# Issuing the stores of gates and of block one's split weight parts from GpSimd's queue, in a one-core streaming encoder layer

## The chip, the cores and the metric

The kernel runs on one core of one Trainium2 chip. The metric is device time of one execution in microseconds; lower is better. The profile calls the engines PE (TensorE's matmuls), PEld (TensorE's weight loads), DVE (VectorE), ACT (ScalarE), POOL (GpSimd) and SP (SyncE, which here only issues transfers). A "q" behind a name, as in SPq, is that engine's queue of instructions.

## The reference

One layer of a chunk-causal encoder on a prompt of 2048 frames and a sample of 64 frames, width 1024, all in fp32. Cut to what matters:

```python
h = rms_norm(x, p['norm1_g']) * (1 + sc1) + sh1
z = h @ p['w_in']
glu_a, glu_b, q, k, v, g_conv, g_attn = jnp.split(z, offs, axis=-1)
u = glu_a * jax.nn.sigmoid(glu_b)
conv_out, conv_state = conv_module(u, ...)      # causal depthwise conv, 31 taps; layer norm; swish; projection
q, k = rms_norm(q), rms_norm(k)                 # per head
attn_out = attend(q, k, v, rel_bias) @ p['w_attn_out']   # each chunk of 64 sees itself and 8 before it
merged = jax.nn.sigmoid(g_conv) * conv_out + jax.nn.sigmoid(g_attn) * attn_out
x = x + gt1 * (merged @ p['w_o'])
h2 = rms_norm(x, p['norm2_g']) * (1 + sc2) + sh2
gate, up = jnp.split(h2 @ p['w_ffn_in'], 2, axis=-1)
x = x + gt2 * ((jax.nn.silu(gate) * up) @ p['w_ffn_out'])
```

Shifts, scales and gates (sh, sc, gt) come from a small conditioning vector. The states of convolution, keys and values are outputs too.

## The kernel before, in words

**Precision.** Products are made in a fast 32-bit format. Each fp32 operand is split into a high part, a copy rounded to that format (`whi`, made on ACT), and a low part, the rest (`wlo`, a subtraction on DVE or POOL); three products, high by high, high by low and low by high, are summed in PSUM (`mm3`).

**Two phases.** The first phase walks over four blocks of tokens (`PBLOCKS`, 576 then three times 512). In each block TensorE makes, in this order: queries, one part of the gated convolution input, keys, another part, values, two more parts, and then the 16 columns of gates (`ORDER`). Attention of the block runs in between. Results that the second phase needs go to DRAM: queries, keys, values, attention (`o_d`), convolution (`c_d`) and the gates (`g_d`). The second phase walks over three blocks (`CBLOCKS`), merges, projects and runs the feed-forward part, with seven products of half-size blocks in place of eight.

**Weights.** Class `Weights` hands out the split weights in the order of use. A raw weight is loaded into a staging buffer (`wst`, three of them at first), split into `whi` and `wlo` (five pairs are held), and used. Weights that a later block uses again, those of the first phase and five of the feed-forward part (`KEPT`), are split once: `then` at lines 511 to 517 stores both parts to DRAM (`w_din_h`, `w_din_l`, `w_dqkv_h` and so on; the store is line 515), and the later blocks load them back (line 480). A part's pair of buffers is free again when TensorE has used it and its store has landed. The store is written down a little after the split (`stream.at`).

**Gates.** `gates` at lines 1389 to 1421 makes each gate column in parts of 288 tokens (block zero), or of 512 or 256: eight or more products into a PSUM bank, a tanh on ACT into a buffer of the tag `t` (seven buffers, lines 776 to 779, which other temporaries share), and a store into `g_d`, line 1399. The second phase loads the gates at line 1133.

**What sets the order.** TensorE's order is written out by hand: the program walks through the work with a running estimate of each engine's load (`Stream`, `Meter`) and interleaves several lists of work (`Lane`). `Meter` lets `dma_start` through without counting it. The other queues are filled by the framework from this program; every queue then runs in order. An instruction that waits holds up what stands behind it in the same queue. SP's queue holds nearly all transfers: loads of weights (line 385 and line 480), of queries and keys for attention (1464, 1465), of values (1471, 1473), of the attention bias (1517), of rows of x for the next block's norm (1146 and 1159), and stores of convolution results (1363), attention (1495), keys and queries (1026), values (1053). ACT's queue holds its own activations and the gates' stores. POOL's queue holds no transfer before the change. Its work in the first phase: the root `r` of the norms of queries, keys and rows of x (`rsqrt_mean`), the sums `s` of the convolution's norm, copies of the convolution's history (`hist`), and some low parts of weights (`wlo`).

Every operation that the program issues through `Meter` has line 106 in the profile; so groups there are told apart by the names of the tiles.

Of the kernel before, what the change touches and what calls it, by code (L numbers as in the profile page):

```python
# [8 lines left out]
F32 = mybir.dt.float32  # L9
# [54 lines left out]
KEPT = ("qkv", "in", "fi")  # L64
# [205 lines left out]
class Weights:  # L270
# [4 lines left out]

    def __init__(self, engines, pool, dram, stream, keys, source, staging, held, kept):
        self.stream = stream
        self.sync, self.act, self.dve, self.gps = engines
        self.pool, self.dram, self.keys, self.source = pool, dram, keys, source

        self.staging, self.held, self.reach = staging, held, 0
        self.sum_pool, self.sum_d, self.sums, self.early, self.landed = None, None, {}, False, {}
        self.behind = nullcontext

        self.room, self.leaving = {"wst": 1, "wup": 0, "wfo": 0}, {"wst": 0, "wup": 0, "wfo": 0}
        times, raws = {}, {}
        self.items, self.users, self.need, self.first, self.stored, self.spread = [], [], {}, set(), {}, set()

        def item(key):
            self.items.append(key)  # L290
            self.users.append(0)
            return len(self.items) - 1

        for i, key in enumerate(keys):
            n = times[key] = times.get(key, 0) + 1
            if key[0] == "up" and n == 1:
                self.first.add(i)
                cs = [c for f, op in key[1:] for c in self.columns_of(f, op)]
                for c in cs:
                    if c not in raws:  # L300
                        raws[c] = item(("fi", c))
                self.need[i] = sorted({raws[c] for c in cs})
                for f, op in key[1:]:
                    for c in self.parts_of(f, op):
                        self.users[raws[c]] += 1
            elif key[0] == "dn":
                fs = [key[:3], (*key[:2], key[2] + 1)]
                for f in fs:
                    if f not in raws:
                        raws[f] = item(("fo", f[2]))  # L310
                self.need[i] = [raws[f] for f in fs]
                for op in key[3:]:
                    for e in self.rows_of(op):
                        self.users[raws[fs[e]]] += 1
            elif n == 1 or not kept(key) or n == 2 and key[:2] == ("qkv", 0):
                self.need[i] = [item(key)]
                self.users[self.need[i][0]] += 1
                if key[0] == "fo" and key[1] in last_rows(0) and n == 1:
                    self.spread.add(self.need[i][0])
        self.raws = raws  # L320
        self.again = {key for key, n in times.items() if n > 1 and kept(key)}
        self.loaded, self.ready, self.used, self.freed, self.given = {}, [], 0, 0, 0

        self.extra = {"wst": staging - 1, "wup": 1, "wfo": 2}

        self.tags = {"fo": (), "": ("wst", "wup", "wfo")}
        self.due = {kind: [] for kind in self.tags}
        for i, key in enumerate(self.items):
            self.due[self.kind(key)].append(i)
        due = self.due[""]  # L330
        for c in (0, FFN):
            due.remove(raws[c])
            due.insert(due.index(self.need[keys.index(("fi", 3 * P))][0]), raws[c])
        self.load_on("")
# [130 lines left out]
    def split(self):  # L465
        i = len(self.ready)
        key = self.keys[i]
        its = self.need.get(i, ())
        if key[0] == "dn":
            shape = [P, len(key) - 3, 512]  # L470
        elif i in self.first:
            shape = [P, 4 * len(key) - 4, P]
        else:
            shape = list(self.loaded[its[0]][0].shape) if its else self.stored[key][1]
        hi = self.pool.tile(shape, F32R, tag="whi", name="whi", bufs=self.held)
        lo = self.pool.tile(shape, F32R, tag="wlo", name="wlo", bufs=self.held)
        self.ready.append((hi, lo))
        if not its:
            for t, d in zip((hi, lo), self.stored[key][0]):
                self.sync.dma_start(t.bitcast(F32), d)  # L480
            return
        turn = {"wo": key[1], "fi": key[1] // P if key[0] == "fi" else 0}.get(key[0], 0)

        passing = key[:2] == ("qkv", 0) and i < 4
        on_dve = ( key[0] == "in" or key[0] == "qkv" and (passing or key[1]) or turn % 2)
        if key[0] == "dn":
            parts = [(slice(j, j + 1), self.second(key, op)) for j, op in enumerate(key[3:])]
            self.stream.after("act", "pool")
        elif i in self.first:
            parts = [(slice(4 * j, 4 * j + 4), self.operand(f, op)) for j, (f, op) in enumerate(key[1:])]  # L490
            self.stream.after("act", "pool")
        else:
            n = 4 if key[0] == "fi" else shape[1]
            parts = [(slice(j, j + n), self.loaded[its[0]][0][:, j : j + n]) for j in range(0, shape[1], n)]
        for c, src in parts:

            late = key[0] in ("up", "fo") and key[1] != (0, "s1") and self.stream.load["pool"] - self.stream.load["pe"] > POOL_BEHIND
            e, name = (self.dve, "dve") if on_dve or late else (self.gps, "pool")
            self.act.activation(hi[:, c], src, AF.Copy)
            self.stream.after(name, "act")  # L500
            e.tensor_tensor(lo[:, c], src, hi[:, c].bitcast(F32), ALU.subtract)
        if i in self.first:
            its = [self.raws[c] for f, op in key[1:] if op[0] == "a" for c in self.parts_of(f, op)]
        if key[0] == "dn":
            its = [self.raws[*key[:2], key[2] + int(op[1]) - 1] for op in key[3:] if op[0] == "b"]
        for j in its:
            self.drop(j, name)
        if key[0] == "dn" and key[3] == "b11":
            self.sum_second(key)

        def then():
            if key in self.again and key not in self.stored and not passing:
                ds = [self.dram.tile(shape, F32, name="w_d" + "_".join(map(str, key)) + "_" + part) for part in "hl"]
                for t, d in zip((hi, lo), ds):
                    self.sync.dma_start(d, t.bitcast(F32))
                self.stored[key] = ds, shape
            self.presum()

        self.stream.at(self.stream.when(name), then, True)
# [104 lines left out]
def streaming_layer(ctx: ExitStack, tc: tile.TileContext, I, O):  # L624
    nc = tc.nc
    stream = Stream()
# [762 lines left out]
    def gates(b, free):  # L1389

        o = PBLOCKS[b][0]
        w = PBLOCKS[b][1] - o

        def part(g, ws, c0, c1):
            ps = columns(*ws, kts(hh), kts(hl), c0, c1)
            t = temp("gate")
            stream.after("act", "pe")
            act.activation(t[:, : c1 - c0], ps[:, : c1 - c0], AF.Tanh, scale=0.5)
            nc.scalar.dma_start(g_d[g // 8, g % 8, :, o + c0 : o + c1], t[:, : c1 - c0])

        def pair(g):
            ws = [W.get(("in", 2560 + g * P, h)) for h in range(2)]
            return [[[w[l][:, k, e * P : e * P + P] for w in ws for k in range(4)] for l in range(2)] for e in range(2)]

        n = 16 - SPLIT_G if b + 1 < len(PBLOCKS) else 16
        for g in range(0, n, 2):
            for e, ws in enumerate(pair(g)):
                for c in halves(0, w):
                    part(g + e, ws, *c)
                if e:  # L1410
                    W.done()
                    W.done()
                yield g + e
        rest = [ws for g in range(n, 16, 2) for ws in pair(g)]
        for c0, c1 in ((0, w // 2), (w // 2, w)):
            for i, ws in enumerate(rest):
                part(n + i, ws, c0, c1)
                if c1 == w and i % 2:
                    W.done()
                    W.done()  # L1420
            free["columns"] = c1
# [265 lines left out]
    M = Slabs(nc.sync, nc.scalar, wa, stream, list(mod_order()), source, 4)  # L1687
    xs = first_columns()
    next(vectors_)
    W = Weights((nc.sync, act, dve, gps), wpool, dram, stream, list(weight_order()), source, 3, 5, lambda key: key[0] in KEPT)  # L1690
    M.fill()
    ordered = ExitStack()
    ordered.enter_context(tc.manual_schedule(engines={mybir.EngineType.PE}))
# [259 lines left out]
    c0, c1 = tile_chunks(*CBLOCKS[0])  # L1953
# [517 lines left out]
```

## Time and profile before

| What | us |
|---|---|
| runs of the kernel before, median of 3 | 2938.12 (2931.04 to 2940.68) |
| the profiled execution, its own time | 2935.84 |
| its span | 2934.1 |
| PE busy in the span | 2877.2 |
| DVE, ACT, POOL busy | 2044.7, 1366.9, 1170.4 |

The profiled execution is one run; its own time holds the span and about 1.7 us around it. Busy time counts when an engine works, not when it works at its best. "Idle before, releaser" names what ended an idle stretch. Where a wait needs several events, the one that came last is named, and it is inferred.

### The profile page before, as it was taken

Reading aid. Unit: us, or ns where it says so; the run is one execution under the profiler, and the core shown is the slowest. Engines: PE = TensorE matmul, PEld = TensorE weight load, DVE = VectorE, ACT = ScalarE, POOL = GpSimd, SP = SyncE. Lnnn points to the kernel's source line nnn. Section 1 sums busy time; section 2 is a strip of 40 time slices with the busy share of each in tenths; the row PEclk is TensorE's granted clock in tenths of the full one; section 3 lists DMA queues with packets and bytes.
Section 4 is the critical chain, followed back from the end, with each engine's and each line's share of the span. In section 5 each row is a group of like instructions: output and inputs, shape, how many; then the busy total and the mean of one; then the engine's idle time right before and its main releaser. Section 6 shows DMA issues by size and latency. Waiting matters only on the chain.

```text
span 2934.1 us, 44538 instructions
## 1 busy us (share of the span) xinstructions
PE 2877.2 (98%) x16130; PEld 2578.7 (88%) x16130; DVE 2044.7 (70%) x3621; ACT 1366.9 (47%) x2441; POOL 1170.4 (40%) x742
## 2 busy tenths in 40 slices
PE   8998999999999999999999999999999999999999
PEld 6798878788888888898999998999999999999998
DVE  5995688578867886487777756666666557566666
ACT  4345634661465267464434345444444345444442
POOL 1301310101011102454566452366667742465767
PEclk9998999999999999999999999999999999999999
DMA  8989889988997897884444876232333965333333
GB/s 320 331 299 320 278 284 307 288 282 288 292 309 233 298 272 238 287 311 166 147 144 144 290 253 215 94 125 87 115 123 104 344 223 180 97 101 108 115 107 127
DMA packets 313788, 634.28 MB, mean 216 GB/s; under 512 B 36864, under 2 KB 133664, under 8 KB 313568
## 3 DMA queue, kind: packets, MB, share of 16 engines
q1 hardware_dynamic: 300464, 612.88, 63.3%
q10 hardware_dynamic: 13104, 18.56, 1.8%
q8 instruction: 127, 2.08, 0.3%
q14 instruction: 93, 0.76, 0.1%
HBM read 482.81 MB, written 148.51 MB: 215 GB/s over the span
## 4 chain that ended last, share of the span: by engine, by line
PE 48%; DVE 2%; ACT 1%; issue 0%; POOL 0%; ACTq 0%; DVEq 0%
PE ps L106 29%; PE pd L106 14%; PE pw L106 5%; DVE wlo L106 1%; DVE pw L106 0%; ACT whi L106 0%; DVE ps L106 0%; DVE t L106 0%; DVE sums L106 0%; PE pt L106 0%; DVE acc L106 0%; ACT xn L106 0%; DVE hid L106 0%; ACT hid L106 0%; DVE b L106 0%
## 5 line engine op out<-in xcount | busy, mean ns | idle before, releaser
L106 PE MATMUL ps<-t,whi 128*128 128x384 f32 (+1 forms) x2112 | 502.1, 322 | 2.1 <-ACT u L106 0.8
L106 POOL TENSOR_TENSOR wlo<-wst,whi 128x1024 fp32r<-128x1024 f32 (+1 forms) x159 | 363.2, 2296 | 239.9 <-ACT whi L106 204.8
L106 ACT ACTIVATE whi<-wst 128x1024 fp32r<-128x1024 f32 (+1 forms) x265 | 257.9, 978 | 294.4 <-PE ps L106 126.7
L106 PE MATMUL ps<-b,whi 128*128 128x384 f32 (+1 forms) x1584 | 378.4, 324 | 4.8 <-DVE v L106 2.1
L106 PEld LDWEIGHTS ps<-t,whi 128*128 128x128 f32 x2112 | 367.6, 188 | 9.5 <-ACT u L106 3.0
L106 DVE SCALAR_TENSOR_TENSOR y<-u,wd,y 128x512 f32<-128x512 f32 (+1 forms) x480 | 369.3, 773 | 7.7
L106 PE MATMUL ps<-hh,whi 128*128 128x512 f32 (+2 forms) x992 | 364.2, 367 | 0.0
L106 DVE TENSOR_TENSOR acc<-acc,pd 128x512 f32<-128x512 f32 x482 | 322.3, 685 | 48.6 <-PE pd L106 46.1
L106 PE MATMUL ps<-hh,wlo 128*128 128x512 f32 (+2 forms) x992 | 346.3, 349 | 0.0
L106 PE MATMUL ps<-hl,whi 128*128 128x512 f32 (+2 forms) x992 | 345.9, 349 | 0.0
L106 PE MATMUL ps<-t,wlo 128*128 128x384 f32 (+1 forms) x1056 | 338.2, 321 | 0.0
L106 PE MATMUL pd<-whi,hid 128*128 128x512 f32 x912 | 297.3, 391 | 0.3 <-DVE hid L106 0.3
L106 PEld LDWEIGHTS ps<-b,whi 128*128 128x128 f32 x1584 | 275.6, 188 | 12.9 <-DVE v L106 3.2
L106 ACT ACTIVATE pr<-pr,sm 128x640 f32<-128x640 f32 (+3 forms) x272 | 202.5, 749 | 154.4 <-DVE sm L106 152.3
L106 PE MATMUL ps<-b,wlo 128*128 128x384 f32 (+1 forms) x792 | 255.0, 322 | 0.0
L106 POOL TENSOR_TENSOR r<-t,mhalf 128x8 f32<-128x8 f32 (+4 forms) x54 | 86.3, 1599 | 395.6 <-DVE t L106 385.4
L106 PEld LDWEIGHTS ps<-hh,wlo 128*128 128x128 f32 x992 | 188.0, 189 | 23.1
L106 PEld LDWEIGHTS ps<-hh,whi 128*128 128x128 f32 x992 | 188.6, 190 | 17.3 <-issue 2.5
L106 PEld LDWEIGHTS pd<-whi,hid 128*128 128x128 f32 x912 | 171.1, 188 | 36.3 <-ACT hid L106 0.7
L106 DVE TENSOR_TENSOR wlo<-wst,whi 128x1024 fp32r<-128x1024 f32 (+1 forms) x106 | 134.5, 1276 | 97.6 <-ACT whi L106 96.4
L106 PEld LDWEIGHTS ps<-hl,whi 128*128 128x128 f32 x992 | 188.9, 190 | 14.8 <-issue 1.7
L106 PEld LDWEIGHTS ps<-t,wlo 128*128 128x128 f32 x1056 | 198.1, 188 | 0.8
(235 smaller groups left out, 6274.6 us busy)
## 6 DMA issues: line engine op xcount, KB each, us to landing
whi<-w_din_h SPq DMA_DIRECT2D x72, 512.0 KB, 6.1
wlo<-w_din_l SPq DMA_DIRECT2D x72, 512.0 KB, 6.9
wst<-sum_d SPq DMA_DIRECT2D x131, 256.0 KB, 2.9
wfo<-in_w_ffn_out SPq DMA_DIRECT2D x64, 512.0 KB, 3.9
sum_d<-ws SPq DMA_DIRECT2D x88, 256.0 KB, 2.2
wst<-in_w_ffn_in SPq DMA_DIRECT2D x85, 256.0 KB, 2.9
wst<-in_w_ca SPq DMA_DIRECT2D x35, 512.0 KB, 5.2
wst<-in_w_ffn_in SPq DMA_DIRECT2D x35, 512.0 KB, 4.6
```

The costliest lines, as they stand in the source:

```text
L106: self.last = f(*args, **kw)
```

## The change

Two groups of stores are issued from another queue. The stores of both parts of a weight that is used again (line 515) move from SP's queue to GpSimd's; the stores of the gates (line 1399) move from ACT's queue to GpSimd's. Sources, destinations, sizes and the arithmetic stay the same. `Weights` gets the plain GpSimd engine as a fifth engine, beside the metered one.

```diff
-        self.sync, self.act, self.dve, self.gps = engines
+        self.sync, self.act, self.dve, self.gps, self.other = engines
...
                 for t, d in zip((hi, lo), ds):
-                    self.sync.dma_start(d, t.bitcast(F32))
+                    self.other.dma_start(d, t.bitcast(F32))
...
             act.activation(t[:, : c1 - c0], ps[:, : c1 - c0], AF.Tanh, scale=0.5)
-            nc.scalar.dma_start(g_d[g // 8, g % 8, :, o + c0 : o + c1], t[:, : c1 - c0])
+            nc.gpsimd.dma_start(g_d[g // 8, g % 8, :, o + c0 : o + c1], t[:, : c1 - c0])
...
-    W = Weights((nc.sync, act, dve, gps), wpool, dram, stream, list(weight_order()), source, 3, 5, lambda key: key[0] in KEPT)
+    W = Weights((nc.sync, act, dve, gps, nc.gpsimd), wpool, dram, stream, list(weight_order()), source, 3, 5, lambda key: key[0] in KEPT)
```

## The prediction, made before the changed kernel ran

> **What bounds the kernel now.** I read the page first, then the stages, then what TensorE waits for, and last the queue that the moved stores stand in now (SP) and the one that they go to (GpSimd's, which the profile calls POOL). The stages below come from the windows view: stretch, its length, busy time of PE, weight loads, VectorE (DVE), ScalarE (ACT) and POOL, then the granted clock, the DMA share and GB/s.
>
> ```profile
> span 2934.1 us, 44538 instructions
> PE 2877.2 (98%) x16130; PEld 2578.7 (88%) x16130; DVE 2044.7 (70%) x3621; ACT 1366.9 (47%) x2441; POOL 1170.4 (40%) x742
> ```
> ```profile
> 50.00:335.00 285.00, 270.62 (x1744) 246.82 (x1744) 227.77 (x415) 136.01 (x270) 66.20 (x48) 0.97 0.92 313
> 335.00:1171.00 836.00, 816.32 (x4417) 682.40 (x4416) 627.59 (x1214) 417.88 (x768) 98.73 (x82) 0.99 0.88 282
> 1171.00:1340.00 169.00, 163.63 (x1006) 148.31 (x1006) 108.41 (x210) 94.82 (x168) 90.20 (x54) 1.00 0.82 282
> ```
>
> TensorE sets the time: it is idle for 2934.1 - 2877.2 = 56.9 us in all, and no change of queues can win more. All moved stores lie before 1340 us, where TensorE is idle for 14.4 us in 50 to 335 us (block zero), 19.7 us in 335 to 1171 and 5.4 us in 1171 to 1340. In the first two stretches the 16 DMA engines are 0.92 and 0.88 busy, so a transfer that is issued sooner still shares them. POOL is free for most of the time there: 66 of 285 us, then 99 of 836. Who waited for whom, with total, times and the longest, says for TensorE:
>
> ```profile
> PE sc L106 <- DVE sm L106: 9.5, 5, 4.0
> PE pt L106 <- DVE kn L106: 8.7, 4, 4.2
> PE pt L106 <- POOL r L106: 7.2, 1, 7.2
> PE sc L106 <- DMA kk<-k_d: 4.1, 3, 2.3
> ```
>
> These largest waits are few and short: attention scores (sc) waiting for the softmax before them or for keys (kk), and transposes (pt) waiting for a normalised row (kn) or for the root r of the next block's norm, which POOL computes. So POOL itself stands in two of these chains.
>
> **The change part by part.** First, the stores that leave SP and ACT (an issue's ns, min/median/max, and the first and last start).
>
> ```profile
> L515 SPq DMA_DIRECT2D w_din_h<-whi x24: 319/506/1819, 50.9 to 285.4; - x24
> L515 SPq DMA_DIRECT2D w_din_l<-wlo x24: 319/432/1141, 51.4 to 286.2; - x24
> L515 SPq DMA_DIRECT2D w_dqkv_h<-whi x12: 424/556/1922, 61.8 to 329.2; - x12
> L515 SPq DMA_DIRECT2D w_dqkv_l<-wlo x12: 320/472/999, 62.2 to 329.7; - x12
> L515 SPq DMA_DIRECT2D w_dfi_h<-whi x5: 326/932/1068, 1270.7 to 1288.3; - x5
> L515 SPq DMA_DIRECT2D w_dfi_l<-wlo x5: 422/444/1032, 1275.8 to 1289.3; - x5
> ```
> ```profile
> L1399 ACTq DMA_DIRECT2D g_d<-gate x84: 326/326/359, 182.7 to 1170.8; - x84
> ```
>
> 82 issues leave SP. By the medians they are 24 x 0.506 + 24 x 0.432 + 12 x 0.556 + 12 x 0.472 + 5 x 0.932 + 5 x 0.444 = 41.7 us of its queue, 34.9 us of it before 330 us. 84 issues leave ACT, 84 x 0.326 = 27.4 us. ACT is 47% busy and none of those largest waits names it, so this is worth nothing: ACT's idle time covers it.
>
> The gate stores hold SP up too, though SP doesn't issue them:
>
> ```profile
> SPq L1464 <- DMA g_d<-gate: 23.9, 8, 7.6
> ...
> SPq L1473 <- DMA g_d<-gate: 2.7, 1, 2.7
> ```
>
> These are the first and the last of 11 such rows, in all 42 waits and 110.2 us. Line 1464 loads queries and line 1473 loads values; neither touches g_d. I read this as completions that are counted together, so that a load waits for a store it has nothing to do with; the profile only infers releasers, so this is a reading. If the gate stores are counted apart, these waits go. SP is not on the end's path, so I count only where a late load reaches TensorE:
>
> ```profile
> 253.88 0.61 SPq L1464 DMA_DIRECT2D q<-q_d  x1
> 259.10 0.46 SPq L1465 DMA_DIRECT2D kk<-k_d  x1
> ...
> 266.95 0.42 SPq L515 DMA_DIRECT2D w_din_h<-whi  x1
> 267.43 0.43 SPq L515 DMA_DIRECT2D w_din_l<-wlo  x1
> 267.95 2.69 SPq L1517 DMA_DIRECT2D bias<-in_rel_bias  x2
> ...
> 274.60 0.33 SPq L515 DMA_DIRECT2D w_din_h<-whi  x1
> 275.22 0.32 SPq L515 DMA_DIRECT2D w_din_l<-wlo  x1
> 276.19 0.50 SPq L1146 DMA_DIRECT2D x_t<-in_x_prompt  x1
> ```
> ```profile
> 275.36 0.29 DVE L106 CUSTOM_DVE_ANT_0 pr<-sc,bias 128x128 f32<-128x128 f32 x1 [3.59 <-DMA bias<-in_rel_bias]
> ```
> ```profile
> 283.41 1.06 ACT L106 ACTIVATE x_t<-x_t 128x1024 f32<-128x1024 f32 x1 [5.05 <-DMA x_t<-in_x_prompt]
> ```
> ```profile
> 275.72 0.79 PE L106 MATMUL sc<-kk,q 128*128 128x256 f32 x2 [3.96 <-DVE sm L106]
> 285.92 0.48 PE L106 MATMUL pt<-ident,r 128*128 128x128 f32 x1 [7.24 <-POOL r L106]
> ```
>
> SP stands still from 254.49 to 259.10, 4.6 us, before the load of keys. Two weight stores go ahead of the bias load at 267.95; it lands late, the softmax waits 3.59 us and TensorE 3.96 us. Two more go ahead of the load of x_t at 276.19; ACT waits for it until 283.41, the root r follows, and TensorE idles 7.24 us. For the bias I take the whole 3.96 us, since the 4.6 us and the two issues (0.85 us) that leave are more than the wait. For x_t: from 274.60 on, two issues and what they wait for take 1.6 us up to 276.19. Two stores of 512 KB also lie ahead of it in its queue, 1.05 MB at 313 GB/s, 3.4 us; on another queue they still share the engines, so I take half, 1.7 us. That gives 3.3 of the 7.24 us, and ACT's other work is late next. Of the 4.1 us for keys I take half, 2.0 us, for the waits on gate stores. Gain: 3.96 + 3.3 + 2.0 = 9.3 us, between 0 (the engines were the limit) and 3.96 + 7.24 + 4.1 = 15.3 us.
>
> Second, what arrives at POOL: 166 issues, 72 + 32 of them before 335 us (32: block zero's 16 gates in two halves each). No row of before has a DMA issued from POOL. The lower bound is ACT's 0.326 us for the same gate store, the upper one POOL's own smallest frequent work:
>
> ```profile
> L106 POOL TENSOR_TENSOR r<-t,mhalf 128x8 f32<-128x8 f32 x32 | 70.1, 2191 | 234.2 <-DVE t L106 234.1
> ```
>
> 2.19 us. Between them I take their geometric mean, 0.85 us, since the operation is the first row's and the engine the second's. 104 x 0.85 = 88 us, added to 66 us in 285, leaves POOL idle for 131 us there. The Trainium skill, "DMA: Bandwidth & Descriptors", section Latency and other measured facts, puts the first byte of a DMA from this queue at about 1 us against about 0.6 us from the hardware queues; by that 104 issues would take some 104 us, an estimate from that page.
>
> What counts is what an issue stands in front of. POOL computes r for each row of queries and keys:
>
> ```profile
> 102.44 8.48 POOL L106 TENSOR_TENSOR r<-t,mhalf 128x8 f32<-128x8 f32 x1 [3.69 <-DVE t L106]
> 113.78 7.75 POOL L106 TENSOR_TENSOR r<-t,mhalf 128x8 f32<-128x8 f32 x2 [2.86 <-DVE t L106]
> ```
> ```profile
> 112.94 0.63 PE L106 MATMUL pt<-ident,kn 128*128 128x128 f32 x4 [1.83 <-DVE kn L106]
> ```
>
> Here TensorE waits already (the other kn wait of this stretch is of the same kind), and weight parts are stored in this stretch too. With one pair of stores ahead of each of the two rows, r is late by 2 x 0.85 = 1.7 us twice: 3.4 us lost, from nothing (the stores fall behind) to 2 x 2 x 2.19 = 8.8 us. At 1270 to 1290 us ten issues, 8.5 us, fall into a stretch in which POOL works nearly without a break:
>
> ```profile
> 1302.66 1.30 POOL L106 TENSOR_TENSOR ws<-wfo,ws 128x512 f32<-128x512 f32 x1 [7.93 <-DMA sum_d<-ws]
> ```
>
> POOL idles 7.93 us right after it, which takes up all but 0.6 us; without that cover it is 8.5 us. Waits of a store for its own data are new on POOL: behind it stand r, the conv sums s and the few weight splits of this stage. SP's order had the same pairs right behind their splits, so I take nothing for this and give the case to a rival.
>
> The sum against the profiled execution, whose own time is 2935.84 us (span 2934.1 us and 1.7 us around it): 2935.84 - 9.3 + 3.4 + 0.6 = 2930.5 us. The median of the runs, 2938.12 us, lies 2.3 us higher, so in its terms 2932.8 us, a gain of 5.3 us. About 0.3%, 8.8 us, is what a measurement of this kernel can tell from no change.
>
> **The rivals.** (a) More comes back: all 15.3 us, and POOL's issues hide: 2938.1 - 15.3 = 2922.8 us. For it speaks SP's 110.2 us of waits, which delay everything in its queue; against it the 0.92 of the DMA engines.
>
> (b) Nothing comes back, because the transfers are the limit in this stage, whatever queue they are in: the bytes stay the same, x_t lands when the engines have moved what is ahead of it, and the two small costs (4.0 us) are half hidden. 2938 to 2942 us. The 0.92 speaks for it, SP's still stand against it. The Trainium skill says the same in "DMA: Bandwidth & Descriptors", section Issuing engines are not separate DMA queues: issuing from several engines saves only sequencer time. By that rule alone the change is worth nothing; the rows on SP's waits show sequencer time that is not small.
>
> (c) Slower: a gate store stuck in POOL's queue.
>
> ```profile
> POOL s L106 <- DVE y L106: 311.9, 11, 54.3
> ```
>
> POOL waits 28.4 us on average, at most 54.3 us, for the convolution's taps on VectorE. A gate store that is queued behind such a wait keeps its buffer, one of 7 of the tag t. The issues of 200 to 250 us give the rate and, last, the us to landing:
>
> ```profile
> g_d<-gate ACTq DMA_DIRECT2D x13, 144.0 KB, 5.1
> ```
>
> One gate each 50 / 13 = 3.8 us fills 7 buffers in 27 us; less the landing, a wait of more than 22 us stops ACT, its PSUM bank and TensorE. The longest alone would cost 54.3 - 22 = 32 us: 2938.1 - 5.3 + 32 = 2964.8 us. Against it: if a store is queued where its data is ready, it stands ahead of these waits.
>
> (d) Slower: POOL's issues stretch as its r did. The two rows above took 8.48 us for one r and 7.75 us for two, where its mean is 2.19 us, while VectorE ran without a gap. If an issue stretches to 7.75 / 2 = 3.9 us, the two pairs cost 4 x 3.9 = 15.6 us, and the late stores eat the gain: 2938.1 + 15.6 = 2953.7 us. The Trainium skill, "SBUF — State Buffer", section SBUF: two separate sides, warns that a DMA from GpSimd can't get its descriptors written while VectorE runs certain two-port operations; the stretched r agrees that the two engines disturb each other here, but no run here shows it for a DMA.
>
> **How the numbers follow.** My forecast, 2932.8 us, gets 0.45; its own range is 2926 to 2938 us, which the 0.3% bound of 2929.3 us parts into 0.21 faster and 0.24 the same. Rival (a) gets 0.15, faster. Rival (b) 0.17, the same. Rivals (c) 0.12 and (d) 0.11, slower. Together: faster 0.36, the same 0.41, slower 0.23. The range that leaves out a tenth at each end reaches from the lower part of (a), 2921 us, to (d), 2954 us.
>
> **What would show it right or wrong.** Right: SP's waits on g_d<-gate are gone; the bias wait before the score at 275 us is gone and the wait on r near 286 us is at most 4 us; TensorE's waits on kn grow by some 3 us; POOL's issues last about 0.85 us. Wrong by (b): the 3.96 and 7.24 us stand as before. By (c): ACT's gates wait for a gate store, and TensorE for ACT's gates, between 182 and 330 us or in a later gate stage. By (d): issues of several us on POOL between 50 and 130 us, and kn waits of 10 us or more. TensorE's idle time after 1340 us should stay as it is; a change there would be none of my causes.

## The result, and the profile after

The changed kernel takes 2959.07 us, the median of 4 runs (2957.11 to 2964.21); beside it the kernel before takes 2935.05 us (4 runs, 2931.04 to 2940.68). The ratio is 1.0084, with a 95% interval of 1.0069 to 1.0099: slower by 24 us. That is outside the predicted range of 2921 to 2954 us, and on the other side of no change.

From the page of the changed kernel, the span and the first of the engines' busy times:

```profile
span 2959.2 us, 44724 instructions
PE 2887.9 (98%) x16130; PEld 2587.1 (87%) x16130; DVE 2054.6 (69%) x3621; ACT 1364.2 (46%) x2441; POOL 1252.5 (42%) x908
```

TensorE is idle for 2959.2 - 2887.9 = 71.3 us, 14.4 more than before, and it is busy for 10.7 us more with the same 16130 products. So over a third of the loss is no idle time at all; the last section comes back to that. The windows view, with the columns and stretches of the prediction:

```profile
50.00:335.00 285.00, 265.92 (x1703) 242.37 (x1702) 220.47 (x399) 130.70 (x263) 107.89 (x147) 0.96 0.90 312
335.00:1171.00 836.00, 814.57 (x4383) 679.97 (x4382) 635.11 (x1221) 412.48 (x762) 125.23 (x133) 0.99 0.87 279
1171.00:1340.00 169.00, 157.64 (x947) 142.82 (x946) 103.75 (x193) 89.28 (x155) 93.41 (x63) 0.97 0.79 273
```

TensorE lost in the first and in the last stretch, and POOL grew by 42 us in the first one. What TensorE waits for (total, times, longest):

```profile
PE sc L106 <- DVE sm L106: 16.9, 10, 8.0
PE pt L106 <- DVE kn L106: 11.5, 3, 4.5
PE ps L106 <- DVE t L106: 5.8, 4, 3.6
PE ps L106 <- DMA whi<-w_dqkv_h: 3.6, 2, 2.7
PE ps L106 <- DVE wlo L106: 3.3, 1, 3.3
```

The 3.96 us for the bias are gone, as forecast. The 7.2 us for r are gone as well, of which I had forecast 3.3. Others stand in their place. None of the five rows names POOL, and none names a gate.

A row of waits doesn't say when time is lost. TensorE's order is the same in both traces up to 1287 us of the kernel before, and again from 1323 us on, so I subtracted the start of each product before from the start of the same product after. This delay (worked out from the two traces; left, the time in the kernel before) gives the places, here with four of the experiments below:

| at us of before | after | order held | order only | keys early | norm early |
|---|---|---|---|---|---|
| 90 | 0.0 | 0.3 | 1.6 | 5.8 | -1.9 |
| 118 | 4.3 | 0.2 | 11.7 | 15.2 | -1.6 |
| 172 | 9.4 | 0.2 | 14.1 | 15.3 | -1.5 |
| 200 | 21.5 | 4.1 | 30.4 | 15.2 | 8.6 |
| 270 | 23.2 | 4.1 | 30.5 | 15.2 | 8.6 |
| 300 | 8.3 | -4.9 | 18.7 | 15.4 | -1.1 |
| 880 | 5.8 | -4.1 | 12.7 | 17.1 | -2.5 |
| 1260 | 17.0 | -0.5 | 14.6 | 19.1 | -2.2 |
| 1335 | 24.7 | 3.9 | 17.6 | 19.8 | -1.4 |
| 2900 | 24.7 | 3.8 | 17.2 | 19.7 | -1.8 |

After: 23 us are lost up to 270 us, 15 come back by 300 (more than the 9.3 that I had forecast), then 11 us go between 880 and 1260 and nearly 8 up to 1335. Behind that nothing happens.

The early losses, first the two largest of TensorE's rows in the timeline of the changed kernel (start, length, what, and in brackets the wait before it):

```profile
103.57 0.69 PE L106 MATMUL pt<-ident,kn 64*128 64x64 f32 x4 [4.52 <-DVE kn L106]
...
193.88 0.79 PE L106 MATMUL sc<-kk,q 128*128 128x256 f32 x2 [8.00 <-DVE sm L106]
```

Who made them late is not POOL. ACT's rows in the same timeline:

```profile
91.03 0.63 ACT L106 ACTIVATE part_h<-cache 128x512 fp32r<-128x512 f32 x1 [8.55 <-DMA q_d<-part_h]
...
167.79 1.06 ACT L106 ACTIVATE whi<-wst 128x1024 fp32r<-128x1024 f32 x1 [10.00 <-DMA wst<-in_w_gate]
...
184.01 1.06 ACT L106 ACTIVATE x_t<-x_t 128x1024 f32<-128x1024 f32 x1 [9.44 <-issue]
...
191.36 1.06 ACT L106 ACTIVATE x_t<-x_t 128x1024 f32<-128x1024 f32 x1 [4.96 <-DMA x_t<-in_x_prompt]
```

ACT squares rows of x for the next block's norm here (x_t), and its weight splits and softmax stand behind them. "Issue" in the third row says that the profile names no releaser; the row's load, issued at 171.24 us, lands at 183.94. VectorE makes the low part of the weight behind it, and the softmax that TensorE waits for at 193.88 us comes after that in VectorE's queue:

```profile
186.14 1.23 DVE L106 TENSOR_TENSOR wlo<-wst,whi 128x1024 fp32r<-128x1024 f32 x1 [7.93 <-ACT whi L106]
```

In the kernel before the four squares stand between 259 and 283 us. SP's queue has their loads earlier too; the first row is from before, the others are from after:

```profile
249.65 3.63 SPq L1146 DMA_DIRECT2D x_t<-in_x_prompt  x3
```
```profile
76.44 0.33 SPq L1053 DMA_DIRECT2D v_d<-vst  x1
76.86 0.47 SPq L1026 DMA_DIRECT2D q_d<-part_h  x1
...
83.02 0.64 SPq L1464 DMA_DIRECT2D kk<-q_d  x1
...
86.30 0.38 SPq L1026 DMA_DIRECT2D q_d<-part_h  x1
...
150.35 11.01 SPq L1053 DMA_DIRECT2D v_d<-vst  x3
163.81 0.33 SPq L385 DMA_DIRECT2D wst<-in_w_gate  x1
164.25 0.37 SPq L1146 DMA_DIRECT2D x_t<-in_x_prompt  x1
```

The x_t loads come 85 us earlier. A store of values (v_d), which waits for its data, now stands ahead of the stores of queries (q_d); three more, 11 us from the first to the last, stand ahead of the loads of gate weights. The change touches none of these instructions. Set side by side, the two programs differ in more than the moved stores. With these left out, the two traces have another instruction in 156 places of SP's order, 249 of ACT's, 288 of VectorE's and 31 of POOL's, though VectorE issues no store at all. TensorE's order differs too, in 145 places between 1287 and 1323 us: it is written out by hand only in the first phase (up to line 1768). The framework fills the queues from a schedule of its own, and with 166 stores gone from SP and ACT it came out differently.

**Theory A**: the loss is this re-sorting of in-order queues, not the new place of the stores. **Rival B**: the stores cost it where they now are (issue on POOL, and what queues behind). **Rival C**: their transfers do, from the new queue.

### The profile page after: what moved, and what is told of

Read it like the earlier page. It is cut to its first block, busy times and chain, and to the rows that moved or that the text cites. A ratio compares the mean times of both kernels' runs of the same rounds, so it can differ in the third digit from the quotient of the medians.

```text
span 2959.2 us, 44724 instructions
## 1 busy us (share of the span) xinstructions
PE 2887.9 (98%) x16130; PEld 2587.1 (87%) x16130; DVE 2054.6 (69%) x3621; ACT 1364.2 (46%) x2441; POOL 1252.5 (42%) x908
## 4 chain that ended last, share of the span: by engine, by line
PE 48%; DVE 2%; ACT 1%; issue 1%; POOL 0%; ACTq 0%; DVEq 0%
PE ps L106 29%; PE pd L106 14%; PE pw L106 5%; DVE wlo L106 1%; DVE pw L106 0%; ACT whi L106 0%; DVE ps L106 0%; DVE t L106 0%; DVE sums L106 0%; PE pt L106 0%; DVE acc L106 0%; ACT xn L106 0%; DVE hid L106 0%; ACT hid L106 0%; DVE b L106 0%
## 5 line engine op out<-in xcount | busy, mean ns | idle before, releaser
L106 POOL TENSOR_TENSOR wlo<-ws,whi 128x512 fp32r<-128x512 f32 x95 | 125.7, 1343 | 169.2 <-ACT whi L106 169.2
```

Of the source, the lines that this page charges most:

```text
L106: self.last = f(*args, **kw)
```

## The experiments

All of them are compared with the kernel before, run beside them on the same chip; its medians there are 2933.8 to 2934.9 us. Where an order is held, the order of the named engines' instructions in one built program is recorded and imposed on another, as an order of issue without any wait (cut):

```diff
         streaming_layer(tc, ins, outs)
+        hold_order(tc, nc)
...
+def hold_order(tc, nc):
...
+            if prev is not None:
+                tc.add_manual_dep(i, prev, mybir.DependencyInfo(mybir.DependencyClass.NoSync, mybir.DependencyReason.DATA), reason="recorded order")
+            prev = i.name
```

Stores that stand on another engine in the record are left out of it and fall where the framework puts them. In the traces of the first two runs below, what is held stands exactly in the recorded order on all five engines.

**Both moves, order of before held on all engines.** The changed kernel with that edit.

> Both kinds of stores go from GpSimd's queue, as in the changed kernel, but the instructions of TensorE, VectorE, ScalarE and SyncE, and GpSimd's computing ones, keep the order among themselves that they had before. Theory A (the loss comes from the order in which the scheduler put the remaining instructions of SyncE, ScalarE and VectorE once the stores had left them): the waits at 104, 164 and 194 us are gone and the time is 2922 to 2940 us, no slower than before (2935). Rival B (the stores themselves cost it where they now are: their issue on GpSimd, and what queues behind them): 2953 to 2965 us, as the changed kernel. Rival C (their transfers, landing later or crowding the loads from the software queue): 2950 to 2965 us too, with waits on DMA landings in the rows.

Measured: 2935.3 us (10 runs), ratio 0.9998 (0.9987 to 1.001). The loss is gone with all 166 stores on POOL. B and C fall as causes of the 24 us: what the stores cost where they now are, their leaving SP and ACT pays back (the sizes are in the next section). TensorE's waits in this run:

```profile
PE sc L106 <- DVE sm L106: 9.8, 7, 3.2
PE pt L106 <- DVE kn L106: 8.5, 4, 4.1
PE ps L106 <- DVE t L106: 4.8, 5, 1.7
PE pt L106 <- POOL r L106: 4.0, 1, 4.0
PE sc L106 <- DMA kk<-k_d: 2.3, 2, 2.1
```

**No move, order of after.** The kernel before with the order recorded from the changed kernel; its stores stay on SP and ACT.

> The converse: the stores stay on SyncE's and ScalarE's queues as before, but every other instruction keeps the order that it has in the changed kernel. Theory A: 2948 to 2966 us, with the waits near 104, 164 and 194 us back though no store is on GpSimd. Rivals B and C: 2931 to 2941 us, as before.

Measured: 2958.26 us (4 runs), ratio 1.0075 (1.0054 to 1.0096). The loss is there without a single moved store. TensorE's waits (here the largest is 13.4 us, at 204 us):

```profile
PE sc L106 <- DVE sm L106: 22.4, 8, 13.4
PE pt L106 <- DVE kn L106: 12.1, 4, 4.4
PE ps L106 <- ACT kn L106: 4.6, 1, 4.6
```

**Gates alone, and weight parts alone, order free.** One of the two edits of the change at a time:

```diff
-    W = Weights((nc.sync, act, dve, gps, nc.gpsimd), wpool, dram, stream, list(weight_order()), source, 3, 5, lambda key: key[0] in KEPT)
+    W = Weights((nc.sync, act, dve, gps, nc.sync), wpool, dram, stream, list(weight_order()), source, 3, 5, lambda key: key[0] in KEPT)
```
```diff
-            nc.gpsimd.dma_start(g_d[g // 8, g % 8, :, o + c0 : o + c1], t[:, : c1 - c0])
+            nc.scalar.dma_start(g_d[g // 8, g % 8, :, o + c0 : o + c1], t[:, : c1 - c0])
```

> Only the 84 gate stores move to GpSimd; the scheduler orders the rest freely. Up to 200 us it leaves SyncE, ScalarE and VectorE almost as before, and the squares of the next block's norm stay behind. Theory A: no waits at 104, 164 and 194 us, 2924 to 2938 us. Rival B (a price per store on GpSimd, 24 us over 166 stores): half of the loss, 2945 to 2950 us.

> Only the 82 stores of weight parts move to GpSimd; the scheduler orders the rest freely, and it puts the loads and squares of the next block's norm some 85 us earlier and the q_d stores behind the attention's first loads, as in the changed kernel. Theory A: the whole loss, 2950 to 2966 us, with the waits near 104, 164 and 194 us. Rival B: half of it, 2945 to 2950 us.

Measured: gates alone 2939.52 us, ratio 1.0014 (1.0003 to 1.0025); parts alone 2948.22 us, ratio 1.0044 (1.0032 to 1.0056). The totals, 0.14% and 0.44%, fit neither theory well: the parts bring 13 us and not the whole loss that A asked for, and 2948.22 us even lies in the range given for B. The places fit A: with the parts alone the delay is 4.3 us at 118, 22.1 at 200 and 8.3 at 300 us, as in the changed kernel; with the gates alone it is 0.8 us at 200. But the gates lose 7.8 us between 600 and 1000 us, where the parts alone lose 2.4. So both moves re-sort queues, in different stages, and the two losses don't add up to that of both.

**Which queue? SP held; ACT and DVE held; ACT held; DVE held.** The changed kernel each time, with the order of before imposed on the named engines alone (with ACT and DVE together, TensorE's as well).

> Both kinds of stores on GpSimd; only SyncE's own instructions keep the order that they had before (so q_d's stores stand ahead of the attention's first loads, and the x_t loads stand late), ScalarE and VectorE are ordered freely by the scheduler. If SyncE's order is the root of the re-sorted queues (the squares of x_t cannot stand early on ScalarE when their loads stand late): no waits at 104 and 194 us, 2928 to 2942 us. If the order of ScalarE and VectorE costs it by itself: 2948 to 2960 us.

> The other half: TensorE, VectorE and ScalarE keep the order of before, SyncE's is the scheduler's, with the attention's first loads ahead of q_d's stores and x_t loaded early. If SyncE's order alone delays the keys, the wait at 104 us (4.6 us) stays, while the 8.0 us at 194 us go, because the squares of x_t no longer stand ahead of ScalarE's weight splits: 2936 to 2950 us. If both waits stay: 2950 us or more; if both go: 2935.

> Both kinds of stores on GpSimd; ScalarE's computing instructions alone keep the order of before, VectorE and SyncE are ordered by the scheduler. With ScalarE and VectorE held the time was 2942 us, with SyncE held 2961. If ScalarE's order carries the loss (the early copies of the cached values at 85 us, the squares of x_t ahead of the weight splits at 170 to 196 us): 2938 to 2948 us. If VectorE's does (taps ahead of the low parts of weights): 2950 to 2962 us.

> The same with VectorE alone held. If VectorE's order carries the loss: 2938 to 2948 us. If ScalarE's does: 2950 to 2962 us. If each carries a share: both runs lie between 2944 and 2954.

| order of before held on | us | ratio (95%) |
|---|---|---|
| nothing (the change) | 2959.07 | 1.0084 (1.0069 to 1.0099) |
| SP | 2960.97 | 1.0093 (1.0076 to 1.011) |
| DVE | 2952.10 | 1.0064 (1.0043 to 1.0086) |
| ACT | 2941.94 | 1.0028 (1.0014 to 1.0042) |
| TensorE, ACT and DVE | 2941.85 | 1.0032 (1.002 to 1.0044) |
| all | 2935.30 | 0.9998 (0.9987 to 1.001) |

My reading that SP's order is the root falls: with it held alone nothing is won, and the three v_d stores ahead of the gate weights' loads still take 10.7 us there. Holding ACT's order wins about 17 of the 24 us, and holding TensorE's and DVE's besides adds nothing. ACT stands between the loads and everything else: one early instruction that waits for a load holds up splits, softmax and keys behind it, as the rows at 184 and 186 us show. These runs don't part the queues cleanly, as the framework sorts the free ones anew in each: with ACT held, DVE's order differs from before in 154 places and no longer in 288. By subtraction, the last 6.6 us need the order of SP and of POOL's computing as well. The run with SP held shows another thing, POOL's and TensorE's rows:

```profile
266.77 0.57 POOL L1399 DMA_DIRECT2D g_d<-gate  x1 [9.03 <-ACT gate L106]
267.50 0.31 POOL L106 TENSOR_TENSOR s<-s,ln 128x64 f32<-128x64 f32 x1 [0.17 <-issue]
```
```profile
267.87 0.43 PE L106 MATMUL pm<-s,ones 128*128 128x64 f32 x2 [3.61 <-POOL s L106]
```

A gate store waits 9 us for its gate at the head of POOL's queue; the convolution's sum s is behind it, and TensorE waits 3.6 us for that. This is the kind of jam that B means. In the changed kernel its like costs TensorE 1.5 us in all.

**Which instructions?** Two kernels with the stores of before where they were, and one group of instructions put where the changed kernel has it. The edit is `hold_order` again, with the group moved in the record of before; the lists below tell the order and are no code. First the cached values' split on ACT and DVE, v_d and the first loads of keys:

```diff
-SP: q_d q_d | wst | ... | cache_k | ... | v_d kk
+SP: v_d q_d q_d kk cache_k | wst | ...
-ACT: tb tb part_h whi vst
+ACT: tb vst tb part_h whi
```

> The kernel before, its stores where they were, with one group of instructions put where the changed kernel has it: the cached values' split (vst) earlier on ScalarE and VectorE, its store v_d ahead of the first q_d stores on SyncE, and the first loads of keys (kk) and of the key cache ahead of the other q_d stores. If this group alone makes the wait at 104 us (4.5 us, and the lower clock behind it): TensorE waits 4 us or more for kn there and the time is 2938 to 2946 us. If it needs the stores on GpSimd: no new wait, 2932 to 2937 us.

Measured: 2951.39 us (4 runs), ratio 1.0058 (1.0042 to 1.0074): the mechanism, and dearer than I expected. SP's and ACT's rows of this run, then TensorE's:

```profile
81.94 1.15 SPq L1053 DMA_DIRECT2D v_d<-vst  x1
83.53 0.72 SPq L1026 DMA_DIRECT2D q_d<-part_h  x1
```
```profile
90.27 0.69 ACT L106 ACTIVATE part_h<-pt,cols 128x512 fp32r<-128x512 f32 x1 [10.05 <-DMA q_d<-part_h]
```
```profile
106.81 0.50 PE L106 MATMUL ps<-whi,hh 128*128 128x512 f32 x1 [4.62 <-ACT kn L106]
```

v_d goes out at 81.94; q_d behind it is late, its two buffers stay full, ACT waits 10 us for one and everything behind ACT moves. In the changed kernel v_d goes out at 76.44: 4.3 us of delay at 118 us there, 15.2 here. The two weight stores ahead of it here take 0.9 us, so they are not what makes it so late. A load of a raw weight ahead of it waits 12.5 us for a low part (wlo) of a weight. VectorE makes that part at 79.27, behind the values' split, and before that split it idles for 9.5 us. In the changed kernel VectorE makes the same part ahead of the values' split, at 67.25. So this run puts the values' split further forward on VectorE than the changed kernel has it, and its 15.2 us are not the price of the early v_d in the changed kernel.

Then the norm of the next block (the times are the places in the kernel before):

```diff
-SP: x_t x_t x_t at 250, x_t at 276        ACT: squares at 259, 262, 263, 283
+SP: x_t at 159, 168, 170, 173             ACT: squares at 165, and three ahead of the softmax at 176
```

> The kernel before, its stores where they were, with the four x_t loads and their squares alone put about where the changed kernel has them (loads at 159 to 173 us, squares at 165 and ahead of the softmax at 176). If the early norm makes the wait at 194 us and takes away the one for r at 286: TensorE loses 6 to 12 us between 165 and 200, the 7.2 us for r are gone, and the two nearly cancel, 2930 to 2940 us. If squares that early cost nothing by themselves: 2924 to 2930 us.

Measured: 2936.3 us (10 runs), ratio 1.0009 (0.9997 to 1.0022). The table above shows it: 10.1 us lost between 172 and 200 us, 9.7 us regained between 270 and 300. The changed kernel loses 12.1 and regains 14.9 us in these two stretches. So most of its largest loss and of its largest gain are one cause, seen twice, and nearly cancel.

**Attempts at a better one.** With the order of before held, the x_t loads moved forward by about 30 us on SP and each square into a stretch in which ACT idles; with the stores moved, without, and with the ten w_dfi stores left on SP:

```diff
-                    self.other.dma_start(d, t.bitcast(F32))
+                    (self.sync if key[0] == "fi" else self.other).dma_start(d, t.bitcast(F32))
```

> The order of before with both kinds of stores on GpSimd, and the four x_t loads and their squares for the next block's norm moved forward by some 30 us on SyncE and 15 to 25 us on ScalarE, each square into an idle stretch of ScalarE. If the 14 us that the changed kernel regains at 275 to 298 us come from the early x_t: TensorE's wait for r (4.0 us with the order held) goes, and the time is 2928 to 2934 us. If another wait follows right behind it: 2935 us.

> The kernel before, with its stores where they were, and with the x_t loads and squares alone moved forward in the same way. If the early x_t is worth its wait without any store being moved: TensorE's 7.2 us for r go, 2926 to 2932 us. If the gain needs the stores away from SyncE and ScalarE: 2933 to 2937 us.

> As the run with the order held and x_t early, with one edit: the ten stores of the down projection's parts (w_dfi, near 1272 to 1289 us) go back to SyncE's queue. If those ten issues on GpSimd cost TensorE what the window 1260 to 1340 us shows (busy 74.8 us with them, 76.7 to 78.4 without): that window comes back to 76.7 or more and the time is 2 to 3 us less, 2930 to 2933 us. If it is the forward order of that stage or chance: no change, 2934 to 2936 us.

Measured: 2934.88 us, ratio 1.0005 (0.9995 to 1.0015); 2930.48 us, 0.9993 (0.9983 to 1.0003); 2930.43 us, 0.999 (0.9979 to 1.0). With the stores moved the wait for r hardly shrinks (4.0 to 3.6 us). Without, it falls from 7.2 to 0.4 us, but a wait of 4.9 us for the softmax follows at 288 us, and of a gain of 8.1 us at 286 us 3.2 are left by 300. The last is the best of all, 3.7 us below the kernel before, but that is less than the 0.3% that can be told here: no version beats the kernel before clearly. For the w_dfi stores, the windows view of the stretch 1260 to 1340 us (its length, then TensorE's busy time, clock, DMA share, GB/s), with them on POOL and then on SP:

```profile
1260.00:1340.00 80.00, 74.81 (x451) 0.98 0.74 260
```
```profile
1260.00:1340.00 80.00, 77.23 (x481) 1.00 0.78 273
```

77.69 us is what the kernel before has there. By the delay, the stage from 1281 to 1335 us costs 4.8 us with these stores on POOL and about 0.5 with them on SP; in the run with the order held and x_t late it costs 4.4.

**Gates alone, all orders held.**

> Only the gate stores on GpSimd, every other instruction in the order of before, the weight parts' stores on SyncE. If the gain at 275 to 286 us (8.3 us in the run with both kinds moved and the order held) comes from the gates: that gain stays and the costs that came with the parts (4.2 us near 176 us, 2.7 us near 1285 us) go: 2926 to 2931 us. If the gain there comes from SyncE's shorter queue, that is from the parts: 2933 to 2937 us, with TensorE's waits of 4.0 us for bias and 7.2 us for r still there.

Measured: 2935.21 us (11 runs), ratio 1.0007 (0.9996 to 1.0018). Of the bias wait 1.5 us are left, but the wait for r grows:

```profile
PE pt L106 <- POOL r L106: 9.4, 1, 9.4
```

What came early at 275 us is lost at 286. So the gain at r in the run with everything held, 7.2 to 4.0 us, comes with the weight parts leaving SP; the gates bring 2.4 us of the bias wait.

## Why the prediction was wrong, point by point

**The step that failed** is "The sum against the profiled execution": 2935.84 - 9.3 + 3.4 + 0.6. Every term takes rows of the kernel before and removes or adds something, as if SP, ACT, DVE, POOL and TensorE kept the rest of their instructions in the order of those rows; ACT's part is even called worth nothing. In the changed kernel they don't keep it. Held in that order the change measures 2935.3 us against 2934.9; left to the framework, 24 us more; and the new order alone, 23 us more. No rival named this either: (a) to (d) all speak of the moved stores.

**The gains, in the order that they assumed**, were right: bias 3.96 forecast, 4.0 to 0.3 us measured; r 3.94 us to be left of 7.24, 4.0 measured; keys half of 4.1, 2.3 left. Together 3.7 + 3.2 + 1.8 = 8.7 us against 9.3. The row of the bias, with the order held:

```profile
276.12 0.50 PE L106 MATMUL sc<-kk,q 128*128 128x256 f32 x2 [0.27 <-DVE sm L106]
```

SP's 110.2 us of waits on gate stores are gone, too, but for 2.0 us of a load of the gates themselves. That r's wait is gone altogether in the changed kernel is not the merit of the stores alone: the early norm takes most of it away (2.5 us are left in the run with the norm early and no store moved), and pays for it at 194 us.

**The costs** were mis-sized, both of them. An issue on POOL takes 0.53 to 0.57 us in the median of its groups and not 0.85; two of the rows of the changed kernel (min/median/max):

```profile
L515 POOL DMA_DIRECT2D w_din_h<-whi x24: 531/535/772, 49.5 to 295.8; - x24
...
L1399 POOL DMA_DIRECT2D g_d<-gate x84: 539/547/631, 205.3 to 1187.7; - x84
```

With the order held, five of them do stand between two rows of r, as the term of 3.4 us supposed (POOL's rows of that run):

```profile
102.59 8.48 POOL L106 TENSOR_TENSOR r<-t,mhalf 128x8 f32<-128x8 f32 x1 [3.69 <-DVE t L106]
111.03 0.61 POOL L515 DMA_DIRECT2D w_din_h<-whi  x1
111.64 0.53 POOL L515 DMA_DIRECT2D w_din_l<-wlo  x1
112.16 1.58 POOL L515 DMA_DIRECT2D w_dqkv_h<-whi  x3
113.94 5.54 POOL L106 TENSOR_TENSOR r<-t,mhalf 128x8 f32<-128x8 f32 x1 [0.21 <-DVE t L106]
```

Still the kn waits don't grow (8.7 to 8.5 us). The second r starts 0.2 us after its input, as POOL would have idled there anyway. The term of 0.6 us for the down projection's parts is 4.4 us. The cover I named, 7.93 us of idle POOL, lies behind that stage; the stores stand ahead of r and ws inside it. And one cost had no term: 3.9 us near 176 us. There TensorE waits for a softmax that VectorE makes 3.2 us later than before, and VectorE is late because of two waits that the kernel before doesn't have (VectorE's rows with the order held):

```profile
124.73 1.23 DVE L106 TENSOR_TENSOR wlo<-wst,whi 128x1024 fp32r<-128x1024 f32 x1 [1.82 <-ACT whi L106]
136.33 0.75 DVE L106 SCALAR_TENSOR_TENSOR part_l<-pt,cols,part_h 128x512 fp32r<-128x512 f32 x1 [2.42 <-DMA k_d<-part_l]
```

For the first, ACT itself waits for the load of a raw weight (7.9 us at 123.64); the second is named as a wait for a store of keys. Behind them VectorE doesn't idle up to 178 us. The wait itself is 2.2 us; the products behind it run at half clock for some 3 us, by which the delay grows to 3.9. The cost comes with the parts and not with the gates: with the gates alone VectorE has neither wait and TensorE loses nothing there. Why these two transfers land late no run shows. The two costs make 4.4 + 3.9 = 8.3 us against 8.7 of gain, so that the held kernel is no faster. The sum isn't complete: the profiled run of the held kernel lies 5 us above its median, and by the table it loses another 4.4 us between 300 and 1260 us, which the two held runs with early x_t don't.

**What was said to show it.** The kn waits grew by 2.8 us, as I had said they would (3), but not through r on POOL, which takes 2.1 us ahead of the row at 104 us in both kernels: the keys were late through SP and ACT. A sign that comes out right can have another cause; the row at 104 us, not the total, told them apart. TensorE after 1340 us stayed as it was: the delay is 24.7 us at 1335 and at 2900.

**The rivals.** (a) didn't come: with the order held 8.7 of 15.3 us came back, and the stores' costs didn't hide. (b) is what the held order measures in sum, but not by its reason: the waits did move, and other places paid. The Trainium skill, "DMA: Bandwidth & Descriptors", section Issuing engines are not separate DMA queues, says that issuing from more engines saves only sequencer time. By that rule the change was worth nothing, and with the order held it measures 0.9998. (c) named a jam in POOL's queue; the changed kernel shows no wait of TensorE for gates beyond 1.4 us, which stands before too, and the run with SP held shows the jam once, at 3.6 us. (d) isn't seen: the longest issue of any moved store took 0.77 us, not 3.9.

**What stays open.** The losses between 880 and 1260 us (11 us in the changed kernel) I saw in the delay, and that they nearly vanish with ACT's order held; which instructions make them I didn't try. Nor did I try alone what makes the 5.1 us between 118 and 172 us, where ACT waits 10 us for a gate weight. Of the nearly 8 us up to 1335 us, the run with the order held shows 4.4 (the w_dfi stores) and the run with the new order alone, TensorE's included, 3.0. One profile of a kernel can lie 5 us from its median, and that with DVE held lies 10 (2962.02 against 2952.10), so single steps of a microsecond or two in the table are not evidence.

## What to carry to other kernels

Where a framework orders the queues, taking instructions out of one queue re-sorts the others; before you sum up the price of a move, ask what decides the order, and after it, compare the order of all queues before any duration. To tell a move from the re-sorting, impose the old order on the new kernel and the new order on the old one: two runs settle it. And subtract the starts of the same product in both traces: it shows where time goes and comes, and that two large items may be one cause.

## What was not expected of the hardware

A wait cost more here than its length. The windows view of the changed kernel around two of TensorE's waits (length, TensorE's busy time, granted clock, DMA share, GB/s):

```profile
103.00:107.00 4.00, 3.43 (x11) 0.52 0.43 99
107.00:112.00 5.00, 5.00 (x18) 0.70 0.40 97
112.00:118.00 6.00, 6.00 (x38) 1.00 0.86 224
190.00:196.00 6.00, 2.12 (x9) 0.50 1.02 415
196.00:206.00 10.00, 8.75 (x53) 0.86 0.70 233
```

After a wait of 4.5 or 8.0 us the clock is at half and takes several us to return, so the delay behind the 4.52 us wait grew to 7.5 us before slack took part of it back. I put the 10.7 us by which TensorE is busier down to this. No run tried it alone, but the clock's records in the two traces bear it out: half of TensorE's busy time at half clock, an estimate of what that clock cost, is 13.2 us before and 23.7 after, 10.5 us more.

The same price was in the kernel before, around the two waits that went (its window, same columns):

```profile
274.00:291.00 17.00, 8.04 (x32) 0.50 1.00 325
```

Half of the 8.04 us, with the waits of 3.96 and 7.24 us, makes 15.2 us; the changed kernel, at a clock of 1.00 in this window, regained 14.9 there. The forecast had priced these waits at their length alone. The Trainium skill, "TensorE: Matmul & The Clock Gate", section Part 1: The HAM clock gate, has the clock go to half after about 3.4 us of idling and back after as long a stretch of work; 0.52 and 0.50 agree. A forecast should price a wait of that length at up to 1.7 times its length, an estimate from 7.5 / 4.52.

An issue on POOL took about the same for 512 KB (0.533 us in the median) as for 144 KB (0.547 us) with the order free, and the weight parts landed about as fast from POOL's queue as from SP's: 7.3 us in the median with the order held, 7.4 us before.
